# The first layer's modulation sums, begun in block 1's first output products and kept out of two stretches around the layer change

## Chip, cores and metric

The program runs on one core of a Trainium2 chip. The metric is device time of one execution in microseconds (us); three executions of the kernel before gave 2311.14, 2312.92 and 2314.92, median 2312.92.

## What is computed

The reference is two transformer blocks in float32 on 256 tokens of width 1024. Cut to what matters here:

```python
# block 1, layer 0: sliding-window attention and a depthwise convolution, side by side
y = concat([a, (c @ w_pw2) * silu(g_b)]) @ w_out          # "output products", 272 tokens with the 16 meta tokens
h = h + rms_norm(y, ab_post_norm)
# block 1, layer 1: stick-breaking attention
q, k, v, g = split(rms_norm(h) @ sb_w_in)
h = h + rms_norm((sb_attention(q, k, v) * silu(g)) @ sb_w_out)
# block 2, layer l = 0, 1: modulation vectors from one conditioning vector c
mod = (silu(c) @ ada_w[l] + ada_b[l]).reshape(6, D)        # sh1, sc1, g1, sh2, sc2, g2
h = rmsnorm(x, norm_mix[l]) * (1 + sc1) + sh1
# ... l = 0: chunked gating and pooling ("ev"), then the PEER experts; l = 1: differential attention, then PEER
```

The modulation of layer 0 of block 2 is a product of a vector with a 1024 x 6144 matrix. It depends on nothing that block 1 computes, so it can stand anywhere before block 2.

## The kernel before, in words

All engines get their instructions in the order in which the Python code emits them; nothing is reordered. The program goes through stages: `ab_layer` (block 1, layer 0), `sb_layer` (layer 1), `ev_layer` (block 2, layer 0), and on. A stage is made of **units**: a unit takes one weight tile of 512 KB (four 128 x 256 or two 128 x 512 pieces) and runs 16 or 24 matmuls with it. `linear` makes input projections (two units for one pair of accumulators), `linear_o` output products (for each half of the outputs four units, with four accumulators). In `ab_layer` weights go to TensorE (PE) as they are ("n" units). From `sb_layer` on a tile is split (`prep`) into `hi`, written by ScalarE (ACT), and `lo`, the rest, written by GpSimd (POOL) and partly by VectorE (DVE), and three passes are multiplied. `take` prepares one or two units ahead, and `load` asks for weights about four units ahead on SP's queue, into a ring `raw` of four tiles.

After each unit `after_unit` emits what is due: results of the unit before (`pend`, `follow`), one of `hooks` (statistics of the next norm), a step of the attention (`steps`), and then `tick(ns)`: background work. There are two lanes of it, `bgs` with a budget of `ns` for each unit and `bg1` with `self.ns1`; a lane's generator yields the cost of each of its steps, and is advanced while the lane's budget is positive.

The generator `ada` computes the modulation vectors. It loads blocks of 256 rows x 512 columns of `ada_w` (512 KB) into `scratch` and for each block makes two steps: on the first lane a DVE multiply-add over 128 x 512 (L677 the first of a sum, L679 the others), on the second lane an ACT scaling and a POOL add (L675). After eight steps of the first lane a transpose and a reduction follow on DVE (L687, L688), at the end four small matmuls on PE (L695) and an add of the bias (L698). With each second step it asks for a further block (L654), into a ring of three blocks (first lane) or two (second lane), and it starts with three small adds of the identity (L658 to L660) and with loads only. `ada_pool(0, False)` hands out two generators for the first lane (six pieces and two pieces of 512 columns) and one for the second (two pieces); the last two of the twelve pieces are left for a later stage.

In the kernel before the two lanes are filled just ahead of `sb_layer` (L2219, L2220), and each unit there has 1400 ns for the first and 1300 ns for the second. What is left runs in the first units of `ev_layer` (1320 ns each). In `ab_layer` the lanes hold taps of the convolution; `need(0)` in its output products empties them with `drain`, and the rest of these products has no background work. Its result `y` is kept in `scratch`, the tile that holds the blocks of `ada_w` later.

Names used below: `sbr` is the norm factor of `sb_layer`, made on ACT and DVE (L485 to L488) out of a sum on PE; `sbq` (L1164) is its first use, which frees the accumulators of the first two units. `r` and L1373, L1375 are the same in `ev_layer`. `sbo_lo` (L1140) is the low half of the gated attention output, which the output products of `sb_layer` multiply. `psq` and `absq` (ACT; DVE L749) are squares of `y` and their sum, which PE adds up over the partitions at L476.

## Time and profile before

| | us |
|---|---|
| three executions, median (lowest to highest) | 2312.92 (2311.14 to 2314.92) |
| the profiled execution: device time | 2311.26 |
| its span, first to last instruction | 2309.5 |
| PE busy in the span | 2186.9 (95%) |
| DVE, POOL, ACT busy | 1764.0 (76%), 1730.9 (75%), 1291.2 (56%) |
| output products of `ab_layer` | 122.0 to 166.6 |
| `sb_layer`, projections and attention | 172.3 to 333.2 |
| `sb_layer`, output products | 333.2 to 361.0 |
| `ev_layer`, projections | 367 to 428 |

The stages' borders are read from PE's instructions in order of time: L457 are output products, L406 projections. Of the 2309.5 us only the first 430 hold instructions that the change moves. PE is busy in nearly all of it, so a change is worth what it takes from or adds to PE's waits there, and what the granted clock of TensorE does after them.

### The profile page before, as it was taken

How to read it: one execution, taken by the hardware profiler on the slowest of the kernel's cores; microseconds unless marked ns; L12 is line 12 of the kernel's file. 1: busy time of each engine (PE TensorE's matmuls, PEld its weight loads, DVE VectorE, ACT ScalarE, POOL GpSimd, SP SyncE). 2: the span in 40 equal slices, each digit the busy share in tenths (PEclk: the TensorE clock that was granted, in tenths of full speed). 3: DMA queues.
4: the chain of work that ended last, by engine and by line, in shares of the span. 5: the costliest groups of instructions: out<-in, count | busy, mean ns of one | idle time of the engine just before them, and what ended most of it. 6: DMA issues, size and time to landing. Idle time of an engine off the chain costs nothing. (4 is left out here: it accounts for less than half of the span.)

```text
span 2309.5 us, 42025 instructions
## 1 busy us (share of the span) xinstructions
PE 2186.9 (95%) x14729; PEld 1964.3 (85%) x14729; DVE 1764.0 (76%) x3502; ACT 1291.2 (56%) x2608; POOL 1730.9 (75%) x2070
## 2 busy tenths in 40 slices
PE   8988997898999999999999988998999999999997
PEld 7768886898989999887787877998899999888886
DVE  5938888578787999678979776796969997555555
ACT  2435664554437888544444645554458886545454
POOL 1107978788999888876666685579999888777775
PEclk9999999999999999999999989999999999999999
DMA  5327755477878777577888532687878786555554
GB/s 164 110 82 235 238 172 189 134 193 149 172 154 168 156 157 155 174 254 278 306 295 306 171 110 92 195 168 150 165 159 163 156 156 155 196 196 183 200 187 141
DMA packets 285582, 414.88 MB, mean 180 GB/s; under 512 B 16489, under 2 KB 217386, under 8 KB 285370
## 3 DMA queue, kind: packets, MB, share of 16 engines
q1 hardware_dynamic: 279722, 405.30, 64.2%
q10 hardware_dynamic: 5648, 6.89, 1.1%
q8 instruction: 116, 1.90, 0.4%
q14 instruction: 96, 0.79, 0.1%
HBM read 408.98 MB, written 3.15 MB: 178 GB/s over the span
## 5 line engine op out<-in xcount | busy, mean ns | idle before, releaser
L261 POOL TENSOR_TENSOR lo<-raw,hi 128x256 fp32r<-128x256 f32 x956 | 874.9, 944 | 380.1 <-ACT hi L159 369.5
L261 POOL TENSOR_TENSOR lo<-uT,hi 128x256 fp32r<-128x256 f32 x1022 | 779.8, 801 | 80.0 <-ACT hi L159 79.5
L159 ACT ACTIVATE hi<-raw 128x1024 fp32r<-128x1024 f32 x380 | 400.7, 1057 | 422.2 <-DMA raw<-in_peer_v 200.1
L2039 PE MATMUL mm<-h,hi 128*128 128x256 f32 x4096 | 530.9, 282 | 18.8 <-ACT hi L159 17.5
L2039 PEld LDWEIGHTS mm<-h,hi 128*128 128x128 f32 x4096 | 504.4, 189 | 23.1 <-ACT hi L159 20.3
L263 DVE TENSOR_TENSOR lo<-raw,hi 128x512 fp32r<-128x512 f32 (+1 forms) x290 | 224.6, 775 | 237.1 <-ACT hi L159 236.0
L231 DVE STREAM_TRANSPOSE uT<-raw 128x1024 f32<-128x1024 f32 x256 | 316.5, 1236 | 105.1 <-POOL lo L261 78.7
L159 ACT ACTIVATE hi<-uT 128x1024 fp32r<-128x1024 f32 x256 | 271.2, 1059 | 212.0 <-DVE uT L231 196.6
L2039 PE MATMUL mm<-h,lo 128*128 128x256 f32 x2048 | 312.1, 290 | 14.2 <-POOL lo L261 11.5
L2039 PEld LDWEIGHTS mm<-h,lo 128*128 128x128 f32 x2048 | 263.8, 189 | 27.0 <-POOL lo L261 26.6
L2090 PE MATMUL mm<-hi,whi 128*128 128x512 f32 x1024 | 277.4, 392 | 4.0 <-ACT hi L159 3.6
L2090 PE MATMUL mm<-lo,whi 128*128 128x512 f32 x1024 | 275.5, 390 | 0.8 <-POOL lo L261 0.8
L2090 PE MATMUL mm<-hi,wlo 128*128 128x512 f32 x1024 | 274.7, 390 | 1.5 <-DVE wlo L494 1.5
L2090 PEld LDWEIGHTS mm<-hi,whi 128*128 128x128 f32 x1024 | 190.8, 188 | 48.0 <-ACT hi L159 6.9
L2090 PEld LDWEIGHTS mm<-lo,whi 128*128 128x128 f32 x1024 | 191.4, 188 | 43.7 <-POOL lo L261 4.2
L2090 PEld LDWEIGHTS mm<-hi,wlo 128*128 128x128 f32 x1024 | 191.9, 188 | 42.7 <-DVE wlo L494 2.7
L406 PE MATMUL mm<-h,hi 128*128 128x258 f32 (+2 forms) x1344 | 207.1, 297 | 19.8 <-ACT h L159 8.9
L406 PEld LDWEIGHTS mm<-h,hi 128*128 128x128 f32 x1344 | 181.9, 197 | 26.0 <-ACT h L159 9.9
L1942 DVE TENSOR_TENSOR B<-sin,ij 128x512 f16<-128x512 bf16 x256 | 182.8, 751 | 0.0
L159 ACT ACTIVATE A<-B,cos 128x128 f32<-128x128 f16 x512 | 167.9, 403 | 0.0
L494 DVE TENSOR_TENSOR wlo<-slots,whi 128x256 fp32r<-128x256 f32 x192 | 158.1, 824 | 0.6
L406 PE MATMUL mm<-h,lo 128*128 128x258 f32 (+2 forms) x672 | 108.8, 295 | 3.7 <-POOL lo L261 3.1
(480 smaller groups left out, 2763.7 us busy)
## 6 DMA issues: line engine op xcount, KB each, us to landing
raw<-in_peer_u SPq DMA_DIRECT2D x512, 256.0 KB
raw<-in_peer_v SPq DMA_DIRECT2D x128, 1024.0 KB
slots<-in_ada_w SPq DMA_DIRECT2D x56, 512.0 KB
scratch<-in_ada_w SPq DMA_DIRECT2D x40, 512.0 KB
raw<-in_sb_w_in SPq DMA_DIRECT2D x32, 512.0 KB
raw<-in_peer_w_q SPq DMA_DIRECT2D x32, 512.0 KB
raw<-in_od_w_in SPq DMA_DIRECT2D x24, 512.0 KB
raw<-in_ab_w_in SPq DMA_DIRECT2D x22, 512.0 KB
```

Of the source, the lines that this page charges most:

```text
L159: self.nc.scalar.activation(out=out, in_=in_, func=getattr(ACTF, func), **kw)
L231: self.nc.vector.transpose(ut.rearrange("p b c e -> p c b e"), src)
L261: nc.gpsimd.tensor_sub(lo[:, sl], src[:, sl], hi[:, sl].bitcast(F32))
L263: nc.vector.tensor_sub(lo[:, n:], src[:, n:], hi[:, n:].bitcast(F32))
L406: nc.tensor.matmul(ps[mm][:, :T], w[:, o:o + P], x[:, j * 4 + kk, :T], start=(j == 0 and n_of[mm] == 1), stop=(j == nu - 1 and n_of[mm] == ...
L494: nc.vector.tensor_sub(lo, src, hi.bitcast(F32))
L1942: nc.vector.tensor_tensor(out=B.rearrange("p j n i -> p j (n i)"), in0=iota4, in1=ij[:, g].rearrange("p n i -> p (n i)").unsqueeze(1).to_b ...
L2039: nc.tensor.matmul(ps[:, :T], w[:, c * P:(c + 1) * P], x[:, c, :], start=(pas == 0 and c == 0), stop=(pas == 2 and c == KC - 1))
L2090: nc.tensor.matmul(outs[t][d], w[:, t * P:(t + 1) * P], v[:, 512 * d:512 * d + 512], start=(i == 0 and pas == 0), stop=(i == P - 1 and pas ...
```

## The change

The lanes are filled in `need(0)`, right behind `drain`, so the steps start in the output products of `ab_layer`. There the first lane gets 2500 ns for a unit (the second still has 1300), and with `quiet=3` both get nothing in the last three of the eight units. In `sb_layer` both budgets are 0 for the first two units (the first call of `linear`). `y` moves from `scratch` to `hn`, the input of the layer's projections, which nothing reads any more by then. The number of steps, and what is computed, are the same.

```diff
@@ need(j) in ab_layer
                 self.drain()
                 self.hooks += layer_norm(None)
+                self.use_ps("aux")
+                for lane, gens in zip((self.bgs, self.bg1), self.ada0):
+                    lane += gens
@@ ab_layer
-        y = sc[:, :KC * T].rearrange("p (c t) -> p c t", c=KC)
+        y = self.hn
         sq = pool.tile([P, T], F32, name="absq", tag="vT")
         post = self.post_in(y, sq, self.v["ab_post_norm"], T, pool)
-        self.linear_o(2, (ch, None), T, post, need=need)
+        self.linear_o(2, (ch, None), T, post, need=need, ns=2500, quiet=3)
@@ sb_layer
         for e in range(4):
-            self.ns1 = sb1 if e else 1300
             for x, n, f in ((hq, NX, consume_q), (h, T, consume_k), (h, T, consume_v)):
                 first = e == 0 and f is consume_q
-                self.linear(1, x, n, lambda m, ps, e=e, f=f: f(2 * e + m, ps), ns=ns, late=int(first), first=first)
+                self.ns1 = 0.0 if first else sb1
+                self.linear(1, x, n, lambda m, ps, e=e, f=f: f(2 * e + m, ps), ns=0.0 if first else ns,
+                            late=int(first), first=first)
@@ _build
     ada0 = k.ada_pool(0, stage != 99)
+    k.ada0 = ada0 if stage == 99 else ((), ())
...
-                if stage == 99:
-                    k.bgs += ada0[0]
-                    k.bg1 += ada0[1]
                 k.sb_layer(pool)
```

SP's queue in the output products of `ab_layer`, one piece of the difference (`raw_70` and `raw_71` are the halves of the weight ring, `in_sb_w_in` the first weights of `sb_layer`, `in_ada_w` the modulation's):

```order
-L310 DMA raw_71<-in_ab_w_out 128x2x512 x2
+L654 DMA scratch<-in_ada_w 128x2x512
+L310 DMA raw_70<-in_ab_w_out 128x2x512
+L654 DMA scratch<-in_ada_w 128x2x512 x2
+L310 DMA raw_70<-in_ab_w_out 128x2x512
+L654 DMA scratch<-in_ada_w 128x2x512 x2
+L310 DMA raw_71<-in_ab_w_out 128x2x512
+L654 DMA scratch<-in_ada_w 128x2x512 x2
+L310 DMA raw_71<-in_ab_w_out 128x2x512
+L654 DMA scratch<-in_ada_w 128x2x512 x3
 L294 DMA raw_70<-in_sb_w_in 128x4x256 x2
 L294 DMA raw_71<-in_sb_w_in 128x4x256
```

With three more a little ahead of this piece, thirteen blocks of `ada_w` now stand in front of the first weights of `sb_layer`; before there was none.

DVE around the norm factor of `sb_layer`, the kernel before:

```order
L550 TENSOR_TENSOR sq_1167<-sq_1167 128x272
L658 TENSOR_TENSOR scratch<-ident_97 128x32
L659 TENSOR_TENSOR scratch<-scratch,ident_97 128x32
L660 TENSOR_TENSOR scratch<-scratch,ident_97 128x32
...
L485 SCALAR_TENSOR_TENSOR nw_1288<-sbr 128x272
L486 SCALAR_TENSOR_TENSOR nw_1288<-aux_1286,nw_1288 128x272
L488 SCALAR_TENSOR_TENSOR sbr<-nw_1288,sbr 128x272
L1164 SCALAR_TENSOR_TENSOR sbq<-mm_1170,sbr 128x256
```

and the change (L1167 is now the line of `sbq`):

```order
L550 TENSOR_TENSOR sq_1208<-sq_1208 128x272
L485 SCALAR_TENSOR_TENSOR nw_1320<-sbr 128x272
L486 SCALAR_TENSOR_TENSOR nw_1320<-aux_1318,nw_1320 128x272
L488 SCALAR_TENSOR_TENSOR sbr<-nw_1320,sbr 128x272
L679 SCALAR_TENSOR_TENSOR scratch<-scratch,cact_88 128x512
L687 STREAM_TRANSPOSE scratch<-scratch 128x512
L688 TENSOR_REDUCE scratch<-scratch 128x16
L1167 SCALAR_TENSOR_TENSOR sbq<-mm_1211,sbr 128x256
```

The six small adds are gone from ahead of the factor; a step, a transpose and a reduction stand between the factor and its first use, emitted after the third unit.

DVE at the end of `sb_layer`'s attention, the kernel before (from the last gate's input to the last two `sbo_lo`):

```order
L1178 TENSOR_SCALAR gu_2953<-g_2952 128x256
L1186 TENSOR_TENSOR g_2945<-g_2945,gu_2946 128x256
L1136 TENSOR_TENSOR so_2999<-sbgo,g_2945 128x256
L1189 TENSOR_TENSOR sbgo<-g_2952,gu_2953 128x256
L1136 TENSOR_TENSOR so_3003<-aux_2959,sbgo 128x256
L1140 TENSOR_TENSOR sbo_lo<-so_2999,sbo_hi 128x256
L1140 TENSOR_TENSOR sbo_lo<-so_3003,sbo_hi 128x256
```

and the change (lines are three higher):

```order
L1181 TENSOR_SCALAR gu_2974<-g_2973 128x256
L679 SCALAR_TENSOR_TENSOR scratch<-scratch,cact_88 128x512 x2
L1189 TENSOR_TENSOR g_2966<-g_2966,gu_2967 128x256
L1139 TENSOR_TENSOR so_3022<-sbgo,g_2966 128x256
L1192 TENSOR_TENSOR sbgo<-g_2973,gu_2974 128x256
L1139 TENSOR_TENSOR so_3026<-aux_2980,sbgo 128x256
L679 SCALAR_TENSOR_TENSOR scratch<-scratch,cact_88 128x512
L687 STREAM_TRANSPOSE scratch<-scratch 128x512
L688 TENSOR_REDUCE scratch<-scratch 128x16
L1143 TENSOR_TENSOR sbo_lo<-so_3022,sbo_hi 128x256
L1143 TENSOR_TENSOR sbo_lo<-so_3026,sbo_hi 128x256
```

Three steps, a transpose and a reduction have come between. From the first gate's input to the last `sbo_lo` there are now fourteen steps (L677, L679) with two transposes and reductions, where there were five with one. The rest of the output products, which had seven, and `ev_layer`, which had nine with two transposes and reductions, have none. In the middle of `sb_layer` four units have none either, since the second generator of the first lane begins there with its loads.

## Rows read from the trace of the kernel before

**Rows 1.** Two stretches: length; busy (count) PE, PEld, DVE, ACT, POOL; clock, DMA, GB/s.

```profile
122.00:166.60 44.60, 40.92 (x179) 33.31 (x177) 12.21 (x27) 15.81 (x27) 4.03 (x4) 1.00 0.33 107
...
368.00:428.00 60.00, 48.26 (x331) 45.32 (x332) 49.17 (x95) 28.07 (x43) 40.40 (x51) 0.86 0.39 125
```

**Rows 2.** PE in order of time, `ev_layer`: start, us, line, tiles, count, idle before and releaser.

```profile
390.66 2.06 PE L406 MATMUL mm<-h,hi 128*128 128x258 f32 x8 [5.02 <-DVE sb L1375]
...
395.79 1.21 PE L406 MATMUL mm<-h,hi 128*128 128x258 f32 x8
```

**Rows 3.** DVE in order of time, `ev_layer`, around its norm factor `r`.

```profile
381.44 1.21 DVE L679 SCALAR_TENSOR_TENSOR scratch<-scratch,cact 128x512 f32<-128x512 f32 x1
...
386.00 0.94 DVE L485 SCALAR_TENSOR_TENSOR nw<-r 128x256 f32<-128x256 f32 x1
...
387.77 2.34 DVE L679 SCALAR_TENSOR_TENSOR scratch<-scratch,cact 128x512 f32<-128x512 f32 x2
```

**Rows 4.** ACT in order of time, the last ACT instruction of the same factor.

```profile
382.83 0.51 ACT L159 ACTIVATE r<-r,eps 128x256 f32<-128x256 f32 x1
```

**Rows 5.** SP's queue in order of time, the first weights of `sb_layer`.

```profile
155.71 7.70 SPq L294 DMA_DIRECT2D raw<-in_sb_w_in  x3
```

**Rows 6.** ACT in order of time, splitting the second of these weight tiles.

```profile
162.97 1.06 ACT L159 ACTIVATE hi<-raw 128x1024 fp32r<-128x1024 f32 x1 [2.40 <-DMA raw<-in_sb_w_in]
```

**Rows 7.** DVE in order of time, sums of squares in the output products of `ab_layer`.

```profile
152.48 0.44 DVE L749 TENSOR_TENSOR absq<-absq,psq 128x272 f32<-128x272 f32 x1 [0.47 <-ACT psq L159]
...
164.66 1.85 DVE L749 TENSOR_TENSOR absq<-absq,psq 128x272 f32<-128x272 f32 x2
```

**Rows 8.** PE in order of time, the sum over partitions behind these.

```profile
166.57 0.73 PE L476 MATMUL aux<-absq,ones 128*128 128x272 f32 x2
```

**Rows 9.** Stretches of 1 us: length, granted TensorE clock, DMA share, GB/s.

```profile
191.00:192.00 1.00, 1.00 1.04 389
...
194.00:195.00 1.00, 0.50 1.07 359
```

**Rows 10.** PE in order of time, waits in `sb_layer`.

```profile
193.64 1.24 PE L406 MATMUL mm<-h,hi 128*128 128x272 f32 x4 [2.21 <-DVE sbq L1164]
...
221.37 0.70 PE L1241 MATMUL s<-sbq,sbk 64*128 64x256 f32 x2 [0.91 <-DVE z L1247]
...
251.82 0.70 PE L1241 MATMUL s<-sbq,sbk 64*128 64x256 f32 x2 [0.70 <-DVE z L1247]
...
281.80 0.70 PE L1241 MATMUL s<-sbq,sbk 64*128 64x256 f32 x2 [0.38 <-DVE z L1247]
```

**Rows 11.** DVE in order of time, a step, a transpose and a reduction.

```profile
208.36 0.74 DVE L679 SCALAR_TENSOR_TENSOR scratch<-scratch,cact 128x512 f32<-128x512 f32 x1
209.13 0.71 DVE L687 STREAM_TRANSPOSE scratch<-scratch 128x512 f32<-128x512 f32 x1
209.88 0.69 DVE L688 TENSOR_REDUCE scratch<-scratch 128x16 f32<-128x512 f32 x1
```

**Rows 12.** ACT in order of time, the split that stands ahead of `sbr`.

```profile
189.15 1.06 ACT L159 ACTIVATE hi<-raw 128x1024 fp32r<-128x1024 f32 x1 [2.54 <-DMA raw<-in_sb_w_in]
```

**Rows 13.** Waits of PE from 300 to 361 us: us in total, times, longest.

```profile
PE mm L457 <- POOL lo L261: 1.9, 3, 1.1
PE s L1258 <- DVE z L1263: 1.7, 1, 1.7
PE s L1241 <- DVE z L1247: 1.0, 1, 1.0
PE mm L457 <- DVE sbo_lo L1140: 0.4, 1, 0.4
```

**Rows 14.** DVE in order of time, gate units of `sb_layer`.

```profile
312.33 2.08 DVE L679 SCALAR_TENSOR_TENSOR scratch<-scratch,cact 128x512 f32<-128x512 f32 x2
...
330.42 0.18 DVE L698 TENSOR_TENSOR mod<-aux,adab 128x24 f32<-128x24 f32 x1 [2.70 <-PE aux L695]
...
339.34 0.85 DVE L1186 TENSOR_TENSOR g<-g,gu 128x256 f32<-128x256 f32 x1 [0.73 <-ACT gu L159]
```

## Prediction

> **What bounds the kernel now.** I read the page first: TensorE (PE) is busy in 95% of the span, so a change pays only where PE waits. Then the busy times by stretch, to find stages in which PE is not full: in the output products of `ab_layer` it is busy 40.92 of 44.6 us, in the projections of `ev_layer` it works 48.26 of 60 us at a mean granted clock of 0.86 [rows 1]. Then PE in order of time, where each wait names what ended it, and there I read the engine named. Four places matter, in the order of their size here.
>
> In `ev_layer` PE waits 5.02 us for the first use of the norm factor `r`, and then runs slowly: eight matmuls take 2.06 us where they take 1.21 five microseconds later [rows 2]. DVE ends this wait: five ada instructions from 381.44 stand ahead of its part of the factor, which starts at 386.00, and two steps follow from 387.77 ahead of the first use [rows 3], though ACT had its part ready at 382.83 + 0.51 = 383.34 [rows 4].
>
> At the head of `sb_layer` PE waits 2.21 us for `sbq` [rows 10]; behind that the clock stands at 0.50 of full, the 1.2 GHz level, after PE had been nearly idle [rows 9]. What comes late here is a weight tile: ACT stands 2.54 us before the split ahead of `sbr`, for DMA [rows 12]. In the middle three waits of 0.91, 0.70 and 0.38 us recur at the same point of the attention, for DVE's mask add [rows 10]. In the last quarter and the output products PE waits 1.7 and 1.0 us for DVE, 0.4 us for `sbo_lo` and 1.9 us for POOL's `lo` [rows 13].
>
> **The terms.** The sum is made against the profiled execution: 2311.26 us on the device, of which 2309.5 are span. It lies 1.66 under the median, 2312.92; I carry the difference over to the median.
>
> *1. `ev_layer`: -6.3 us.* All nine steps and two transposes with reductions leave. With nothing in front, DVE starts its part of `r` at about 383.34 instead of 386.00 (2.66), and the two steps of 2.34 between factor and first use go: 5.0 together, which is the whole wait. The accumulators come free about when PE wants them. Then PE isn't idle, and the slow unit goes: it began 5.13 before the next one (390.66 to 395.79), where three passes of 1.21 need 3.63, so 1.5. I take 4.8 + 1.5. The later wait on the centred gates follows the units and moves along. Ends: -6.5 (all of both), -4.2 (the 2.66 and the 1.5 alone, if the first use finds something else late, POOL's `lo` first of all).
>
> *2. Border of the two layers: +2.4 us.* This is the new wait that I expect. SP issued the first three tiles of `sb_layer` evenly over 7.70 us: 155.71, 159.37, 163.04 [rows 5]. Now ada blocks stand before them, and a block's issue waits until DVE has used the ring's oldest. The steps that free it stand behind the third sum of squares, done at 152.48 + 0.44 = 152.92 [rows 7]. With steps of 0.74 [rows 11] the next block goes out near 154.3, behind it the last `w_out` tile, two blocks at 155.8 and 157.3, one of the second lane, and the first `sb_layer` tile near 158.2, 2.5 late; the second still at 159.4. That makes seven transfers of 0.524 MB from 154.3 to the second tile. At 389 GB/s [rows 9] each takes 1.35; of the 3.60 that the second tile needed before (159.37 to the split at 162.97 [rows 6]) 2.25 are not transfer. So it lands at 154.3 + 2.25 + 7 x 1.35 = 166.0, not 162.97. ACT has this split in front of the last four squares, and the DVE adds that need them ended at 164.66 + 1.85 = 166.51, 3.54 after it; now 169.5. PE's sum over partitions stood at 166.57 [rows 8], and everything up to the next layer hangs on it: +2.9. At 359 GB/s [rows 9] it is +3.7. At the other end it costs nothing, if the transfers run side by side and the second tile comes through before 163. I take +2.4, nearer the end that the order of the queue makes. PE's last `w_out` tile is issued 2.2 late (154.3 for 152.0) and used three units after, 11 us at the pace of rows 5 (3.67 a unit): hidden.
>
> *3. Head of `sb_layer`: +1.5 us.* The six small adds go from ahead of the factor; DVE waited for ACT there in any case, so nothing comes of it. But a step, a transpose and a reduction now stand between `sbr` and `sbq`: 0.74 + 0.71 + 0.69 and gaps, 2.2 [rows 11], straight on PE's wait. Against it, three ada blocks no longer share the DMA engines with the tile that ACT waited 2.54 for [rows 12]. I take 0.7 for that (ends 0 and 1.9). The half clock behind the wait stays as it is. Ends: +0.3, +2.2. The second lane's steps come earlier here on ACT and POOL; I price them at nothing, since PE's long waits here name DVE and not POOL [rows 10].
>
> The Trainium skill ("DMA: Bandwidth & Descriptors", Queues, rings and completion order) says that each DMA engine consumes one queue's descriptors in ring order. By that rule blocks that stand behind a tile don't hinder it, term 3 is +2.2, and the sum would come out 0.7 higher; the rule speaks against this part of the change. No row here tells which of the two holds: the wait of 2.54 names DMA, but not what the engines moved in it [rows 12].
>
> *4. Middle of `sb_layer`: +0.5 us.* By the new order the wait of 0.91 gets a transpose and a reduction more and an add less in front (1.40 - 0.5 = +0.9); those of 0.70 and 0.38 lose more DVE work than they last and go (-1.08). A wait of 1.8 may bring the clock down, as the 2.21 did: half of 1.5, rounded down to 0.7. Ends: -1.1, +2.4.
>
> *5. Last quarter and output products: +1.4 us.* Fourteen steps stand where five did. Some fall into DVE's waits of 2.70 and 0.73 [rows 14]. At the end most don't: two steps go before L1189, where the 0.73 for ACT was, and cost 1.5 to 2.1 [rows 11, 14], so 0.8 to 1.4 remain; a step, a transpose and a reduction before the last `sbo_lo` add 2.1 to 2.4. Together 2.9 to 3.8, say 3.3, on PE's wait of 0.4. POOL's three waits of 1.9 in all [rows 13] lie behind and take up that much, since POOL doesn't wait for PE there: 1.4 remain. Half the cost of a slow unit (0.8) comes on top. Off go 0.8: the gate units begin with an emptier DVE, and the waits of 1.0 and 1.7 shrink by 0.4 each. Ends: -1.5 (the two waits nearly gone, `sbo_lo` hidden), +4.5 (3.8 and the slow unit, little taken up).
>
> In the output products of `ab_layer` fifteen steps of 0.74, 11 us, fall on a DVE that is busy 12.21 of 44.6 us [rows 1]: nothing, while PE is fed. `y` in another tile costs what it did.
>
> Sum: -6.3 + 2.4 + 1.5 + 0.5 + 1.4 = -0.5. On the profiled execution 2310.8, on the median **2312.4**.
>
> **Rivals.** *Faster.* The `ev_layer` gain stands whole (-6.5) and the new waits hide: the second tile lands by 163.3 (+0.3), `sbr` comes 1.4 earlier (+0.8), middle -0.2, last quarter 0. Sum -5.6: 2307.3. For it: DMA is busy a third of the output products [rows 1], and the budget stops three units before the border. Against it: SP takes its instructions in order, and thirteen blocks are a lot.
>
> *Slower.* DVE becomes the bound of the gate units. PE waits 1.7 and 1.0 for it there already [rows 13]. Nine steps more at 1.04 (2.08 for two [rows 14]) with 1.4 for transpose and reduction are 10.8; less its pauses of 3.4 [rows 14], 7.4 are left, with one slow unit 8.9, and if POOL is held up as well nothing is taken up. That is 7.5 above term 5: 2319.9. It decides once the steps there take over about 1 us each. Against it: four units before have no steps, so DVE enters with less behind it.
>
> **How the numbers follow.** A measurement of this kernel can tell about 0.2%, 4.6 us, from no change, so below 2308.3 is faster and above 2317.5 slower. The forecast, a gain in `ev_layer` given back at the border and by the stick-breaking layer: 0.47. The faster rival: 0.32, because term 2 rests on an estimate of seven transfers and is the one most easily too high. The slower one: 0.21. The forecast alone covers 2308.3 to 2317.5; the range takes in most of the faster case (terms 1 and 2 at their good ends with 3 to 5 as taken give 2309.8, with 5 at its good end 2306.9) and the nearer half of the slower: 2305.5 to 2318.5.
>
> **What would show it.** Term 1: no L677 or L679 in `ev_layer`, and a wait for the first use under 0.5 us, with the clock full after it. Term 2: splits of the first two `sb_layer` tiles at 164 to 166 and PE's sum at L476 two to three us later against the start of the output products. Term 3: PE waits 3 to 4 us for `sbq`. Term 4: one longer wait for the mask add, two gone. Term 5: a wait of about 3 us for `sbo_lo`, and POOL's waits smaller. The forecast is wrong if the splits come by 163.5, or if the gate units wait over 6 us for DVE in all, or if `ev_layer` keeps its wait, since then another engine held the first use.

## The result, and the profile after

The change makes the kernel slower: 2323.2 us median (2320.12 to 2328.84, 10 runs) against 2309.19 (2301.98 to 2315.3, 10 runs of the kernel before on the same chips), ratio 1.0061, 95% interval 1.0046 to 1.0076, about 14 us. The profiled execution of the changed kernel has a span of 2320.9 us, that of the kernel before 2309.5.

First the page's line of busy times, then four instructions of PE in order of time that begin a stage (start, us, engine, line, operation, tiles, count, idle before and what ended it): the first output product of `ab_layer`, the first projection of `sb_layer`, the first of `ev_layer`, the first output product of `ev_layer`. Kernel after:

```profile
PE 2195.1 (95%) x14729; PEld 1972.7 (85%) x14729; DVE 1761.7 (76%) x3502; ACT 1291.8 (56%) x2608; POOL 1724.3 (74%) x2070
```

```profile
122.83 3.94 PE L457 MATMUL mm<-cat,raw 128*128 128x272 f32 x16
...
185.36 0.80 PE L406 MATMUL mm<-h,hi 128*128 128x256 f32 x2 [4.07 <-ACT h L159]
...
386.44 0.80 PE L406 MATMUL mm<-h,hi 128*128 128x258 f32 x2 [3.94 <-ACT h L159]
...
442.47 0.40 PE L457 MATMUL mm<-ycat_hi,hi 128*128 128x256 f32 x2
```

The same four of the kernel before:

```profile
122.13 3.94 PE L457 MATMUL mm<-cat,raw 128*128 128x272 f32 x16
...
172.27 0.51 PE L406 MATMUL mm<-h,hi 128*128 128x256 f32 x2 [4.06 <-ACT h L159]
...
366.97 0.51 PE L406 MATMUL mm<-h,hi 128*128 128x258 f32 x2 [4.82 <-ACT h L159]
...
428.00 0.40 PE L457 MATMUL mm<-ycat_hi,hi 128*128 128x256 f32 x2
```

The differences of neighbouring starts are the lengths that the rest of the text compares: the **border** (output products of `ab_layer` and the norm behind them) 62.53 us, before 50.14; **`sb_layer`** 201.08, before 194.70; **`ev_layer`** up to its output products 56.03, before 61.03. What lies behind is unchanged and took 1878.43 us, before 1881.50.

One profile of the kernel before is a poor measure for that. Four kernels of the experiments change only `ev_layer`, so with the kernel before there are five profiles of one code for the first two stretches: border 50.14, 53.45, 52.90, 53.43, 50.31 (mean 52.05), `sb_layer` 194.70, 191.03, 191.13, 190.44, 192.38 (mean 191.94). Against these means the change costs 10.5 at the border and 9.1 in `sb_layer`, and gains 5.0 in `ev_layer`: 14.6 together, where 14 were measured. The stretch behind, one code in all of them, took 1871.8 to 1885.3 (mean of the five 1878.1), so a single profile cannot give the 14 as a difference of spans, and the parts, which rest on one profile of the change, are good to a few us: e8 below, with the same code in `sb_layer`, took 205.6 there.

Part of the spread at the border has one place. The unit that begins at about 137 us, L406 `aux<-z,raw`, took 3.8 us from its start to the next unit's in the kernel before and in e15, and 6.4 to 6.8 in the other three and in the change (6.76). Less what exceeds 3.77 there, the five borders are 50.1 to 50.5 and the change's is 59.5: 9.2 us are the change's own, 7.8 up to L476 and 1.5 behind it.

**The border.** In what follows [rows 5 to 8] have their answers. Stretches of the kernel after (length; busy of PE, PEld, DVE, ACT, POOL; clock; DMA share; GB/s):

```profile
149.00:154.00 5.00, 5.00 (x24) 4.14 (x23) 3.41 (x5) 0.87 (x3) 0.00 (x0) 1.00 0.97 341
...
159.00:164.00 5.00, 5.00 (x23) 4.16 (x22) 4.38 (x5) 0.00 (x0) 1.60 (x1) 1.00 0.90 293
164.00:169.00 5.00, 5.00 (x23) 4.16 (x22) 0.00 (x0) 0.00 (x0) 0.00 (x0) 1.00 0.79 242
169.00:173.00 4.00, 1.37 (x6) 0.78 (x5) 0.00 (x0) 0.21 (x1) 0.00 (x0) 1.00 1.01 338
```

SP's queue, and one of its waits from 120 to 200 us (us in total, times, longest):

```profile
152.53 5.67 SPq L654 DMA_DIRECT2D scratch<-in_ada_w  x2
158.25 0.46 SPq L310 DMA_DIRECT2D raw<-in_ab_w_out  x1
161.18 2.46 SPq L654 DMA_DIRECT2D scratch<-in_ada_w  x3
163.73 3.37 SPq L294 DMA_DIRECT2D raw<-in_sb_w_in  x3
```

```profile
SPq L654 <- DVE scratch L679: 9.9, 5, 4.8
```

DVE, POOL and ACT in order of time at the same place:

```profile
157.05 6.47 DVE L679 SCALAR_TENSOR_TENSOR scratch<-scratch,cact 128x512 f32<-128x512 f32 x6
...
176.31 1.84 DVE L749 TENSOR_TENSOR absq<-absq,psq 128x272 f32<-128x272 f32 x2
```

```profile
157.20 3.40 POOL L675 TENSOR_TENSOR scratch<-scratch 128x512 f32<-128x512 f32 x2 [53.27 <-ACT scratch L159]
```

```profile
172.79 1.06 ACT L159 ACTIVATE hi<-raw 128x1024 fp32r<-128x1024 f32 x1 [15.05 <-DMA raw<-in_sb_w_in]
174.24 1.06 ACT L159 ACTIVATE hi<-raw 128x1024 fp32r<-128x1024 f32 x1 [0.40 <-DMA raw<-in_sb_w_in]
175.20 1.24 ACT L159 ACTIVATE psq<-mm 128x272 f32<-128x272 f32 x4
```

PE:

```profile
137.78 6.93 PE L406 MATMUL aux<-z,raw 128*128 128x272 f32 x16 [3.68 <-ACT z L159]
...
178.20 1.28 PE L476 MATMUL aux<-absq,ones 128*128 128x272 f32 x2 [7.83 <-DVE absq L749]
179.27 2.02 PE L476 MATMUL aux<-psq,ones 128*128 128x272 f32 x4
```

Read from the bottom: PE ends its output products and stands 7.83 us for the sum of squares, which DVE ends at 176.31 + 1.84 = 178.15. DVE waits for ACT's last four squares, which are done in one go at 175.20, because ACT stood 15.05 us in front of the split of the first `sb_layer` tile. That tile was asked for at 163.73, 40.90 us after the first output product (before: 155.71 - 122.13 = 33.58), and its split began 9.06 us after the issue (before 159.51 - 155.71 = 3.80), on DMA engines busy 0.79 to 1.01 of the time. SP asked late because ada blocks stood in front and waited for DVE's steps; six of these took 1.08 us each, two POOL adds beside them.

**`sb_layer` and `ev_layer`** after, PE's waits in order of time, for [rows 2, 10, 13]:

```profile
207.72 0.74 PE L406 MATMUL mm<-h,hi 128*128 128x272 f32 x4 [2.39 <-DVE sbq L1167]
...
238.05 0.70 PE L1245 MATMUL s<-sbq,sbk 64*128 64x256 f32 x2 [2.98 <-DVE z L1251]
...
297.14 0.25 PE L695 MATMUL aux<-scratch 128*32 128x8 f32 x8 [2.38 <-ACT sbgo L159]
...
363.86 0.58 PE L457 MATMUL mm<-sbo_lo,hi 128*128 128x256 f32 x1 [2.12 <-DVE sbo_lo L1143]
...
404.86 1.21 PE L406 MATMUL mm<-h,hi 128*128 128x258 f32 x8
...
428.08 2.51 PE L1360 MATMUL s<-wsT,vz 128*128 128x128 f32 x8 [6.23 <-DVE vz L1352]
```

The wait in `ev_layer` for the first use of `r` is gone (404.86), that for the centred gates has grown from 4.28 to 6.23.

### The profile page after: what moved, and what is told of

Read it like the earlier page. It is cut to its first block, busy times and chain, and to the rows that moved or that the text cites. A ratio compares the mean times of both kernels' runs of the same rounds, so it can differ in the third digit from the quotient of the medians.

```text
span 2320.9 us, 42025 instructions
## 1 busy us (share of the span) xinstructions
PE 2195.1 (95%) x14729; PEld 1972.7 (85%) x14729; DVE 1761.7 (76%) x3502; ACT 1291.8 (56%) x2608; POOL 1724.3 (74%) x2070
## 5 line engine op out<-in xcount | busy, mean ns | idle before, releaser
L2043 PEld LDWEIGHTS mm<-h,hi 128*128 128x128 f32 x4096 | 502.9, 189 | 20.7 <-ACT hi L159 18.1
L406 PE MATMUL mm<-h,hi 128*128 128x258 f32 (+2 forms) x1344 | 209.1, 299 | 14.1 <-ACT h L159 8.0
L406 PEld LDWEIGHTS mm<-h,hi 128*128 128x128 f32 x1344 | 183.7, 198 | 20.2 <-ACT h L159 9.4
L406 PE MATMUL mm<-h,lo 128*128 128x258 f32 (+2 forms) x672 | 110.1, 298 | 4.0 <-POOL lo L261 3.6
```

The source lines that it names most:

```text
L406: nc.tensor.matmul(ps[mm][:, :T], w[:, o:o + P], x[:, j * 4 + kk, :T], start=(j == 0 and n_of[mm] == 1), stop=(j == nu - 1 and n_of[mm] == ...
L2043: nc.tensor.matmul(ps[:, :T], w[:, c * P:(c + 1) * P], x[:, c, :], start=(pas == 0 and c == 0), stop=(pas == 2 and c == KC - 1))
```

## The experiments

Each kernel differs from the changed kernel, or where it says so from the kernel before, by the diff shown. Lengths are worked out as above; "blocks" is the number of ada blocks that stand ahead of the first `sb_layer` tile on SP's queue, "wait" what PE waited at L476 ("none": 0.21 us or less). Each row has the lengths of one profile, and the ratio of all its runs. Ratios are against the kernel before.

| kernel | blocks | wait | border | `sb_layer` | `ev_layer` | ratio (95%) |
|---|---|---|---|---|---|---|
| before: five profiles, mean (`ev_layer`: one) | 0 | none | 52.1 | 191.9 | 61.0 | 1 |
| the change | 13 | 7.83 | 62.5 | 201.1 | 56.0 | 1.0061 (1.0046 to 1.0076) |
| e1_quiet6 | 6 | none | 50.4 | 197.8 | 60.0 | 1.0029 (1.0011 to 1.0047) |
| e2_lane1 | 10 | 4.02 | 57.1 | 197.4 | 54.8 | 1.0024 (1.0007 to 1.0041) |
| e3_quiet8 | 2 | none | 53.1 | 197.1 | 61.8 | 1.0023 (1.0009 to 1.0037) |
| e4_budget | 13 | 8.04 | 62.3 | 196.5 | 56.2 | 1.0032 (1.0016 to 1.0048) |
| e5_q6_b1500 | 6 | none | 53.1 | 203.7 | 56.0 | 1.0029 (1.0012 to 1.0046) |
| e6_latesplit | 13 | none | 56.0 | 201.5 | 54.8 | 1.0034 (1.002 to 1.0047) |
| e7_q5_budget | 8 | none | 50.1 | 209.6 | 54.5 | 1.0055 (1.0042 to 1.0067) |
| e8_warm | 13 | 1.49 | 61.3 | 205.6 | 54.5 | one run, no ratio |
| e9_ev_calm | 0 | none | 53.5 | 191.0 | 65.1 | 0.9996 (0.9983 to 1.0009) |
| e10_q6_calm3 | 6 | none | 53.0 | 205.7 | 56.0 | 1.0043 (1.0029 to 1.0058) |
| e11_part | 0 | none | 52.8 | 200.0 | 60.6 | 1.0045 (1.003 to 1.006) |
| e12_ev2000 | 0 | none | 52.9 | 191.1 | 64.9 | 1.0 (0.9983 to 1.0016) |
| e13_ev_aux1600 | 0 | none | 53.4 | 190.4 | 69.3 | 1.0038 (1.002 to 1.0056) |
| e14_both | 13 | none | 53.1 | 195.2 | 54.5 | 0.9997 (0.9979 to 1.0015) |
| e15_ev_late_close | 0 | none | 50.3 | 192.4 | 61.7 | 0.9987 (0.9974 to 0.9999) |

The theory: the loss is made at the border. The chief rival: it is made in `sb_layer`, by where the steps stand there.

### Fewer blocks ahead of the border (e1, e3, e2)

e1 and e3 end the output products' budget earlier (e3: `quiet=8`):

```diff
-                if e == n - 1 and j == nu - quiet:
+                if nu * e + j == nu * n - quiet:
-        self.linear_o(2, (ch, None), T, post, need=need, ns=2500, quiet=3)
+        self.linear_o(2, (ch, None), T, post, need=need, ns=2500, quiet=6)
```

> The change with the budget of the output products ended after their first two units (quiet 6 of 8, not 3): 6 ada blocks, not 13, stand ahead of the first stick-breaking tile on SP. Border theory (the loss is the late split of the first two sb tiles behind ada blocks): PE's sum at L476 comes 0 to 3 us later against the start of the output products than before, not 11, and the time is 0.1 to 0.3% above before (1.001 to 1.003), since the ev_layer gain stays. Rival, the stick-breaking layer itself (ada steps in the way of its mask adds, the two closings of the modulation for one bank): border mended but the layer loses as much, 1.004 or more. Rival, clock only (a half-clock unit in the two small units ahead of the products): those 3 us stay whatever the number of blocks.

> The change with no budget in any of the eight units of the output products; only the two small units ahead of them give some: 2 ada blocks ahead of the first sb tile. Border theory: PE's sum at L476 at its old distance within 1 us; the time 1.000 to 1.003 of before, because the ev_layer steps partly come back. Rival (stick-breaking layer): 1.004 or more all the same, since its first two units are still without budget. With quiet6 this makes a series 13, 6, 2 blocks: the border theory wants the delay at L476 to fall with it.

e2 begins only the first lane early, the second where it began before:

```diff
-                for lane, gens in zip((self.bgs, self.bg1), self.ada0):
-                    lane += gens
+                self.bgs += self.ada0[0]
+                k.bg1 += k.ada0[1]
                 k.sb_layer(pool)
```

> The change with only the DVE lane begun in the output products; the lane of ACT and POOL is begun at the stick-breaking layer as before. 10 ada blocks, not 13, ahead of the first sb tile, POOL's two adds of 1.7 us and ACT's three scales gone from the border. Border theory, by bytes: delay at L476 some 8 us, time 1.003 to 1.005. Border theory, by SP's wait behind the buffers of the second lane: delay falls under 4 us, 1.001 to 1.002. Rival (stick-breaking layer): 1.004 to 1.007.

e1 on SP, ACT and PE, for comparison with the rows above:

```profile
155.66 7.70 SPq L294 DMA_DIRECT2D raw<-in_sb_w_in  x3
```

```profile
163.16 1.06 ACT L159 ACTIVATE hi<-raw 128x1024 fp32r<-128x1024 f32 x1 [2.64 <-DMA raw<-in_sb_w_in]
```

```profile
137.03 3.93 PE L406 MATMUL aux<-z,raw 128*128 128x272 f32 x16 [3.68 <-ACT z L159]
...
166.77 0.72 PE L476 MATMUL aux<-absq,ones 128*128 128x272 f32 x2
```

e2's PE and e3's PE:

```profile
173.52 1.28 PE L476 MATMUL aux<-absq,ones 128*128 128x272 f32 x2 [4.02 <-DVE absq L749]
```

```profile
137.85 6.67 PE L406 MATMUL aux<-z,raw 128*128 128x272 f32 x16 [3.68 <-ACT z L159]
```

With 6 blocks SP asks for the first tile at its old place, the second is split at 163.16, and PE does not wait. The series 13, 10, 6, 2 gives 7.83, 4.02, 0, 0 us: the border theory holds for the border. e2's wait is half of what its version by bytes expected (some 8) and at the edge of the other (under 4), so bytes alone don't set it. The Trainium skill ("DMA: Bandwidth & Descriptors", Queues, rings and completion order) says that an engine consumes a queue's descriptors in ring order; the time from the issue of the first tile to its split, 9.06, 6.58 (e2) and 3.80 us (e1), goes with the blocks issued just ahead of it, as by that rule, though plain sharing of the engines would have the same sign and no run parts the two. The blocks that count are the late ones: in the 3 us ahead of the tile SP issued three in the change, two in e2 and none in e1, and none in e7 either, where 8 blocks stand ahead and the time is 3.68.

But 1.0029 and 1.0023 remain. In e1 `sb_layer` is 5.9 us too long, and `ev_layer` is only 1.0 shorter than before: two steps were left for it, and its closing matmul waited 3.02 us for the reduction behind them. e3 left all nine steps there, and the old wait of 5.0 us stands. The rival is not out. The unit at 137 us shows another thing: after the same idle of 3.68 us it runs slowly in the change (6.93, at a granted clock of 0.50 from 138 to 143 us) and in e3, which has no step there, and at full pace in e1 (3.93, clock 1.00), whose code is that of the change up to there. Those 3 us are not the change's.

### The first two units' budget given back (e4)

```diff
-                self.ns1 = 0.0 if first else sb1
-                self.linear(1, x, n, lambda m, ps, e=e, f=f: f(2 * e + m, ps), ns=0.0 if first else ns,
+                self.ns1 = sb1 if e else 1300
+                self.linear(1, x, n, lambda m, ps, e=e, f=f: f(2 * e + m, ps), ns=ns,
                             late=int(first), first=first)
```

> The change with the budget of the first two units of the stick-breaking layer given back (one part undone; the early begin stays). Border theory: nothing mended, L476 as late as in the change (11 us), time 1.004 to 1.008. Rival (stick-breaking layer, whose steps were pushed together by the two empty units): 1.000 to 1.003.

1.0032, on the edge of the rival's range: the border is as late as ever (8.04), and yet half of the loss is gone. `sb_layer` took 196.5 instead of 201.1, although PE now waited 6.96 us (for a scaling of the second lane on ACT) where it waits for `sbq` otherwise. So there are two losses, and the two empty units are one of them.

### Both at once, with the border mended in two ways (e5, e6, e7, e8)

e5 is e1 with e4's edit and a higher rate in `sb_layer`; e7 is e1 with `quiet=5` and e4's edit, at the old rate.

```diff
-        ns = 1400
+        ns = 1500
```

> The change with the output products' budget ended after two of eight units (6 ada blocks ahead of the first sb tile), the first two sb units given their budget back, and 1500 instead of 1400 per sb unit so that no ada block is left for ev_layer. Two causes (border, and the empty first units of the stick-breaking layer): both mended, the ev_layer gain of about 5 us stays, 0.997 to 1.000 of before. If the border alone is the cause: 1.000 to 1.002, as with quiet 6. If the stick-breaking layer loses whatever the distribution, because ada steps stand in front of its mask adds everywhere: 1.002 to 1.005.

> As the kernel with 6 blocks and the head's budget back, but 8 blocks ahead of the first sb tile (quiet 5) and 1400 per sb unit. The series of blocks is 13, 10, 6, 2 with waits at L476 of 7.8, 4.0, 0, 0 us; by bytes in front 8 blocks should wait 0 to 2 us. Two causes: 0.997 to 1.002 of before. Border alone: 1.001 to 1.003.

e6 keeps the 13 blocks and puts the splits of the first two tiles, ACT's and with them DVE's and POOL's, behind the norm factor:

```diff
-        while self.next_prep <= min(upto, len(self.units) - 1):
+        while self.next_prep <= min(upto, self.hold, len(self.units) - 1):
-        post = self.post_in(y, sq, self.v["ab_post_norm"], T, pool)
+        post = self.post_in(y, sq, self.v["ab_post_norm"], T, pool); self.hold = self.next_take + 9
-        r2 = post.rest()
+        r2 = post.rest(); self.hold = 10 ** 6; self.ahead(self.next_take + 1)
```

> The change with 13 blocks ahead as they are, but the splits of the first two sb tiles put behind the norm factor on ACT, DVE and POOL, so that the last four squares do not queue behind a tile that is late. If it is ACT's order that turns the late tiles into a delay: the wait of 7.8 us at L476 goes (under 1), the first sb product waits for the split instead, 1 to 3 us more than before; net 5 to 8 us against the change, 1.002 to 1.004 of before. If the tiles' lateness counts by itself wherever the splits stand: the same 7 to 8 us stand at the first sb product, 1.005 to 1.007.

e8 has 60 small matmuls ahead of the sum over partitions:

```diff
-        r2 = post.rest()
+        self.warm(60); r2 = post.rest()
```

> The change with 60 small matmuls on PE's way between the last output product and L476, to keep PE busy in the wait of 7.8 us. If the half clock behind the wait is due to PE's standing still: granted clock 1.0 from L476 to the first sb units, L476's six matmuls 1.8 us and not 3.3, and the head 1.5 us shorter. If not: L476 as slow as in the change (matmuls of 1.28 and 2.02 us).

e6's PE at the first projection of `sb_layer`, then e8's PE:

```profile
179.12 0.80 PE L406 MATMUL mm<-h,hi 128*128 128x256 f32 x2 [7.13 <-ACT h L159]
```

```profile
179.71 0.73 PE L476 MATMUL aux<-absq,ones 128*128 128x272 f32 x2 [1.49 <-DVE absq L749]
180.28 1.08 PE L476 MATMUL aux<-psq,ones 128*128 128x272 f32 x4
185.42 0.51 PE L406 MATMUL mm<-h,hi 128*128 128x256 f32 x2 [4.06 <-ACT h L159]
```

e6 shows that it was the place of the splits, ahead of the squares, that turned late tiles into the wait: with the same 13 blocks the wait at L476 is gone, of it 3.1 us come back at the first projection (7.13 for 4.07), and the border is 6.6 shorter than in the change. e8 shows the clock's part: from L476 to the first projection 5.71 us (185.42 - 179.71), in the change 7.16, before 5.70; 1.5 us of the border are the half clock behind PE's standing still. Its time, 2322.42 in one run, does not show it: `sb_layer`, in the same code, took 205.6 us there and 201.1 in the change. Two of its waits were longer, 4.28 for `sbq` and 4.45 at the closing matmul, for 2.39 and 2.38; why, no run shows.

e5 and e7 miss what I expected: the border is free, the `ev_layer` gain is there, and `sb_layer` takes 203.7 and 209.6. In e7 part of the price is paid where my slower rival put it, in the last quarter (1.43 and 1.88 us for `z`, 2.37 for `sbo_lo`) and behind it (3.27 at the sum of squares of the output products), and as much ahead of it: 4.88 for `sbq`, 1.82 and 3.12 for `z`. Both give the first two units their budget back and are longer than e1, by 5.9 and 11.8 us; e5 has a higher rate besides, e7 two more blocks, and both do the steps that e1 leaves for `ev_layer`.

### The last part alone, and a calmer head (e11, e10)

e11: nothing begun early, the first two units without budget, 1500 per unit.

```diff
-                for lane, gens in zip((self.bgs, self.bg1), self.ada0):
-                    lane += gens
+                k.bgs += k.ada0[0]
+                k.bg1 += k.ada0[1]
                 k.sb_layer(pool)
-        ns = 1400
+        ns = 1500
```

> The change's last part alone: nothing begun early, the first two units of the stick-breaking layer without budget, 1500 per unit so that the modulation is done in time; y in hn. Border theory: nothing at L476 (same as before within 1 us); head as before or 1 us better, 0.999 to 1.002. Rival (the empty units push the steps together later): waits for the mask add grow by 3 us or more, 1.002 to 1.005.

e10: e1 and e4, but the first three units without budget (`tick` as in the next section's diff) and 1600 behind them.

```diff
-        ns = 1400
-        sb1 = 1300
+        ns = 1600
+        sb1 = 1300; self.calm = 3
```

> The change with 6 blocks ahead of the first sb tile (border free), and the first three units of the stick-breaking layer without budget, not two, so that no ada step stands between sbr and sbq; 1600 per unit behind them, no block left for ev_layer. If the head's loss is the steps between sbr and sbq: PE's wait for sbq 1.5 to 2.5 us (3.8 with quiet 6), and 0.998 to 1.001. If the layer loses by the number of steps that stand in front of its mask adds, which this raises: 1.002 to 1.005.

e11 has no early block and nothing wrong at the border, and still stands at 1.0045: PE waits 4.59 us for `sbq`, and 3.43, 1.55 and 1.49 for mask adds. The rival's expectation held: empty first units and the higher rate that makes up for them cost by themselves, without any early block; this run doesn't part the two. e10 eases the head, where PE now waits 1.66 us for a split and then 1.09 for the second `sbq`, and loses 13.8 us against the mean in `sb_layer`, by four waits of 1.5 to 2.7 for `z` and two of 1.7 to 2 for `sbo`. Its second expectation held.

### The gain in `ev_layer` alone (e9, e12, e13, e15)

These change the kernel before: three units of `ev_layer` without budget, so that the nine steps come behind `r`.

```diff
-        for i, (lane, n) in enumerate(((self.bgs, ns), (self.bg1, self.ns1))):
+        for i, (lane, n) in enumerate(((self.bgs, ns), (self.bg1, self.ns1)) if self.calm < 1 else ()):
-        self.tick(ns)
+        self.tick(ns); self.calm -= 1
-        self.ns1 = 1300
+        self.ns1 = 1300; self.calm = 3
```

> The kernel before, with nothing begun earlier; only the budget of the first three units of ev_layer is withheld, so that its nine ada steps come behind the norm factor and the first use instead of in front. If the gain that the change sought is the wait of 5.0 us for the first use and the half-clock unit behind it, it is to be had here without the border and without the stick-breaking layer: 4 to 6 us under before, 0.997 to 0.999. If the steps then only move the wait to the gates (two of them now stand ahead of the centred gates' factor) or to the output products: 0.999 to 1.001.

e12, e13 and e15 go on from e9:

```diff
-        self.linear(6, h, T + 2, consume, ns=1320, late=1)
+        self.linear(6, h, T + 2, consume, ns=2000, late=1)
```

```diff
-        self.use_ps("s")
+        self.use_ps("aux")
-        self.linear(6, h, T + 2, consume, ns=1320, late=1)
+        self.linear(6, h, T + 2, consume, ns=1600, late=1)
```

```diff
-        yield 1320
+        yield 2640.0 if (p0, np_) == (6, 2) else 1320
         ps = self.aux_ps()
```

> The kernel before with the first three units of ev_layer withheld from the lanes, as in the run before it, but 2000 instead of 1320 per unit behind them, so that the matmul that closes the modulation stands ahead of the gates' products, where it stood in the kernel before, and not behind them, where PE waited 7.7 us for it. Theory that the ev_layer gain is 5 to 7 us once no new wait takes its place: PE's time at the start of the output products of ev_layer 4 to 7 us earlier against the start of the layer, 0.997 to 0.998 of before. Rival, the steps are pressed in front of the centred gates: the wait there grows from 4.3 by 3 us or more, 0.999 to 1.001.

> The same with 1600 per unit and the closing matmul in a bank of the other kind, between the two gates' products. If the 7.7 us came from the bank that the gates hold: no wait over 1 us for the closing matmul, 0.997 to 0.998 of before. If they came from the closing's own inputs (transpose and reduction late on DVE): a wait of 3 us or more stays, 0.998 to 1.000.

> The kernel before with the first three units of ev_layer withheld (as the first run that changed ev_layer alone) and the matmul that closes the last piece of the modulation one unit later, when the gates have given their bank back. If the 7.7 us there were the wait for a bank whose readers stood behind the closing's own transpose on DVE: the wait goes, PE reaches the output products of ev_layer 4 to 6 us earlier against the start of the layer than before, and 0.997 to 0.999 of before. If the closing waits wherever it stands, or the centred gates take the gain back: a wait of 3 us or more remains in ev_layer beside those of before, 0.999 to 1.001.

PE at the closing matmul, e9 and e15:

```profile
424.60 0.29 PE L695 MATMUL s<-scratch 128*32 128x8 f32 x8 [7.67 <-DVE sv L1361]
```

```profile
420.45 1.13 PE L1395 MATMUL aux<-p,wp 128*128 128x256 f32 x4 [3.27 <-DVE ycat_lo L1401]
421.71 0.25 PE L695 MATMUL s<-scratch 128*32 128x8 f32 x8
```

In all four the wait of 5 us for the first use is gone, and in none is `ev_layer` shorter. The closing matmul waited 7.67 us for a bank (e9), 8.70 for its own reduction (e12), 8.69 for the other bank (e13). In e15 it waits no more, but PE then stands 3.27 us ahead of a pooling product and 6.26 for the gates. e15's 0.9987 is the best figure, inside the 0.2% that a measurement can tell from no change, and its profile shows no gain in the layer. In these four arrangements the 5 us were not to be had while the steps stayed in the layer.

### Border and head mended together (e14)

e6's and e4's edits in one kernel.

> The change with both of its losses mended at once: the splits of the first two sb tiles behind the norm factor, and the first two sb units' budget given back; 13 blocks begun early as in the change. Each alone brought the ratio from 1.006 to 1.003. If the two losses are separate places and add: 0.9995 to 1.0015. If they are the same one seen twice (the head of the stick-breaking layer takes up what the border lets through): 1.002 to 1.004.

```profile
175.11 0.79 PE L406 MATMUL mm<-h,hi 128*128 128x256 f32 x2 [7.14 <-ACT h L159]
...
201.81 2.61 PE L406 MATMUL mm<-h,hi 128*128 128x272 f32 x8 [6.28 <-DVE sbq L1167]
```

0.9997: the two losses add, as the first of the expectations said. Each edit takes away about 0.3%, together the whole 0.6%. What is left of them (3.1 us at the first projection, 4.1 for `sbq`) eats the gain in `ev_layer`, 6.5 us here: the kernel is as fast as the one before, not faster.

Where in `sb_layer` the empty units cost is seen in PE's busy time. The layer's stretch (length; busy of PE, PEld, DVE, ACT, POOL; clock; DMA share; GB/s) in the kernel before, the change and e14 (e4 has 177.25 us of PE at a clock of 0.95):

```profile
172.27:366.97 194.70, 177.22 (x1280) 159.80 (x1280) 160.12 (x266) 113.62 (x194) 161.28 (x181) 0.96 0.65 218
```

```profile
185.36:386.44 201.08, 182.03 (x1288) 165.08 (x1288) 150.54 (x257) 112.53 (x191) 153.98 (x179) 0.93 0.57 185
```

```profile
175.11:370.28 195.17, 177.09 (x1289) 160.24 (x1289) 149.16 (x257) 112.19 (x191) 154.24 (x179) 0.96 0.58 189
```

The five profiles of the code before have 174.8 to 177.2 us (mean 175.5) at a clock of 0.96 to 0.97. The change has eight small matmuls more, and 6.5 us more of busy time: most of its 9.1 us are matmuls that ran slower. In stretches of 1 us the granted clock is at 0.50, the 1.2 GHz level, in five places of the layer in the change and in two or three of the code before; the two that e4 and e14 no longer have lie at 298 and from 363 to 369 us, at the waits of 2.38 for the closing matmul and of 2.12 for `sbo_lo`, and there the first of these waits is gone and the second is 0.49.

## Why the prediction was wrong

The forecast of 2312.4 and its range up to 2318.5 missed 2323.2; "slower" had a chance of 0.21.

*Term 2, the border, is the step that failed:* +2.4 with ends 0 and +3.7; 12.4 against the profile before, 10.5 against the mean of five, 9.2 without the unit at 137 us. The chain was right (blocks ahead, a late split, squares queued behind it on ACT, PE at L476), the sizes were not. "The first `sb_layer` tile near 158.2, 2.5 late": it came 7.3 late against the first output product, of which 3.0 are the half-pace unit. I had priced the steps at 0.74; with the second lane's POOL adds beside them six took 1.08 each, and SP, in order, stood behind them. Of the second lane I had counted a block on the queue here and nothing for its adds; e2, which takes the lane away, has its first five steps at 0.78 and a wait of 4.02, not 7.83. "Seven transfers of 0.524 MB" at 389 GB/s: the number was about right, the time was not. From the block issued at 157.8 (152.53 + 5.67 - 0.37) to the split of the second tile it is 16.4 us, where I had 11.7: 2.0 of the difference lie ahead of the first tile's issue (5.9 for 3.9), 2.7 behind it. The stretches from 149 to 173 us moved 242 to 341 GB/s, not the 389 of one busy microsecond [rows 9]. The half clock behind the new wait, 1.5 us, I had left out here while counting it in terms 4 and 5.

*Terms 3 to 5, `sb_layer`:* forecast +3.4, measured +6.4 against the profile before and +9.1 against the mean. The waits were mostly the named ones; what they do to the clock was too small by far. Terms 4 and 5 had 0.7 and 0.8 for slow units; PE's busy time in the layer grew by 6.5, at the new half-clock places of the rows above.

Term 3 looks right in the two single profiles: from the first projection to the first product behind `sbq` 22.36 us for 21.37, +1.0 where I said +1.5. Over several it is too small: the code before has 21.37, 21.45, 20.50, 20.07 and 20.09 (mean 20.7), the change, e6 and e8, whose steps stand alike at this head, 22.36, 23.64 and 23.84 (mean 23.3), so +2.6, above the end of +2.2. A step, a transpose and a reduction did stand between `sbr` and `sbq`, for 2.6 us (204.55 to 207.16 in the change), since the step took 1.23 and not 0.74. Against it I had taken 0.7 for an earlier tile. ACT waited 0.39 for it in the change instead of 2.54 [rows 12], but 2.13 in e1, 1.31 in e3 and 1.65 in e6, which have no ada block at this head either: the 0.39 is not the blocks' absence alone. By the Trainium skill's rule of ring order ("DMA: Bandwidth & Descriptors", Queues, rings and completion order), which I had set against this part, term 3 would have been +2.2. That is nearer to the +2.6, but the slower step accounts for a part of it, and no run parts them.

Term 4 named the right wait (0.91 grown to 2.98, where I said 1.8; those of 0.70 and 0.38 gone) and missed a new one: two closing matmuls came into one unit, and the second stood 2.38 us for a bank that ACT had yet to empty. Term 5's delay of `sbo_lo` was 2.12 + 0.29, where I said about 3, by just the named instructions:

```profile
360.76 0.81 DVE L679 SCALAR_TENSOR_TENSOR scratch<-scratch,cact 128x512 f32<-128x512 f32 x1
361.60 0.71 DVE L687 STREAM_TRANSPOSE scratch<-scratch 128x512 f32<-128x512 f32 x1
362.35 0.69 DVE L688 TENSOR_REDUCE scratch<-scratch 128x16 f32<-128x512 f32 x1
362.95 1.73 DVE L1143 TENSOR_TENSOR sbo_lo<-so,sbo_hi 128x256 fp32r<-128x256 f32 x2
```

What I priced at nothing and what cost most here is the part with the empty units: e4 against the change, e14 against e6 and e11 (with a higher rate) against the mean give 4.6, 6.3 and 8.1 us of `sb_layer` for it, and the ratios of e4 and e14 bear it out over all their runs. I read them as two units in which nothing can go wrong; with 13 blocks ahead they are two units whose steps come later, among waits. It is no rule: with 6 or 8 blocks ahead the same budget given back went with a longer layer (e5, e7).

*Term 1, `ev_layer`:* -6.3 forecast, -5.0 measured, within the ends. The wait went, and the slow unit too (1.21 at 404.86). But the 1.5 us for that unit came back: "the later wait on the centred gates follows the units and moves along" was wrong. The gates' products start 22.96 us after the first use before (413.62 - 390.66) and 23.22 after (428.08 - 404.86), so the chain behind the first use sets them, not PE's pace, and a faster PE only waits longer, 6.23 for 4.28.

*The rivals:* the faster one needed the border at +0.3, which 8 blocks or fewer have. The slower one named the gate units as the place; e7 shows that place at work in part, the change itself does not. Its time, 2319.9, was nearest, for another reason: that is luck.

*What stays open:* which arrangement of the same steps in `sb_layer` is bad, and why one code takes 201.1 and 205.6 us there. With the border free it took between 195.2 and 209.6 us, and I can name each kernel's waits afterwards but not say them ahead.

## What to carry to other kernels

Background work that is begun earlier puts its loads ahead of the next stage's first weights: count the tiles on the issuing queue at the border, and look which engine has the first use of these weights ahead of something that the critical path needs. Budget that is withheld in one place is spent in another; on an engine that is 84% busy through a stage (DVE: 135.10 of 160.90 us in `sb_layer` before) a step that leaves one wait can land in the next. A wait of PE costs more than its length where the clock falls with it: in `sb_layer` of the change PE stands 2.6 us longer than in the mean of the five, and is busy 6.5 longer. And take several profiles of both kernels: single ones of one code differed by 3.3 us at the border and by 4.3 and 4.5 in `sb_layer`, as much as most terms of a forecast.

## What the runs showed of the hardware that was not expected

A DVE instruction with two inputs in SBUF can stand as long as POOL works without a pause. DVE and POOL of the changed kernel in `ev_layer`, then of e2 in the output products behind it:

```profile
413.41 3.48 DVE L1389 TENSOR_TENSOR pp<-pz 128x256 f32<-128x256 f32 x1 [0.65 <-ACT pz L159]
```

```profile
409.61 7.01 POOL L261 TENSOR_TENSOR lo<-raw,hi 128x256 fp32r<-128x256 f32 x10
```

```profile
457.77 5.37 DVE L527 SCALAR_TENSOR_TENSOR h<-x,gain,h 128x256 fp32r<-128x256 f32 x1
```

```profile
454.56 8.30 POOL L261 TENSOR_TENSOR lo<-raw,hi 128x256 fp32r<-128x256 f32 x12
```

Elsewhere the first takes 0.43 us and the second 0.47. Both end 0.27 to 0.28 us after POOL's run does (416.62 and 462.86). In e2, and with a wait of the same 4.0 us in e1 and e10, PE stood behind it; what it cost in the change the rows don't tell. The Trainium skill ("SBUF — State Buffer", SBUF: two separate sides) says that the port pair which the two engines share is locked for one whole instruction, and the other blocks. The rows agree that DVE blocks; here it stood through a run of several POOL instructions. It is not always so: the six steps at 157.05, with two POOL adds beside them, were only slower (1.08 for 0.74).

The second is the unit at 137 us, which falls to a granted clock of 0.50, the 1.2 GHz level, in some executions of the same code and not in others, after the same idle of 3.68 us: 3.94 us before and 3.93 in e15, 6.96 in e9, all one code there; 3.93 in e1 and 6.93 in the change, one code up to there.
